# A list schedule that keeps VectorE and GpSimd apart on SBUF operands, in a two-layer hybrid encoder

## The chip, the cores and the metric

One core of a Trainium2 chip runs the whole program once. The metric is the device time in microseconds (us) of one execution, the median of several; lower is better. Engines are named as in the profile: PE (TensorE matmuls), PEld (its weight loads), DVE (VectorE), ACT (ScalarE), POOL (GpSimd), SP (SyncE, which issues the DMAs here).

## The reference

Two encoder layers on x of 512 tokens by 1024 features, float32. Cut to what is computed:

```python
for l in range(2):
    x = x + 0.5 * swiglu(rms_norm(x, ffn1_norm[l]), ffn1_w_gate[l], ffn1_w_up[l], ffn1_w_down[l])
    h = rms_norm(x, mix_norm[l])
    pa, pb, pc, pd = jnp.split(h @ w_in[l], IN_SPLITS, axis=-1)
    ya = neighbourhood_mixer(pa, ...)   # 4 heads, 8 x 16 window of an 8 x 64 grid, bias
    yb = mla_mixer(pb, ...)             # 4 heads, low-rank q and kv, rope
    yc = diff_mixer(pc, ...)            # 4 heads, two softmaxes each, T5 bias
    yd = gqa_mixer(pd, ...)             # 4 query heads on 2 kv heads, axial rope
    x = x + jnp.concatenate([ya, yb, yc, yd], axis=-1) @ w_out[l]
    x = x + 0.5 * swiglu(rms_norm(x, ffn2_norm[l]), ffn2_w_gate[l], ffn2_w_up[l], ffn2_w_down[l])
    x = rms_norm(x, final_norm[l])
```

The feed-forward width is 2816.

## The kernel before, in words

Activations lie transposed, features on the 128 partitions and the 512 tokens along the free dimension. Every float32 product is made from float32r operands that are split into a high half (a cast, on ACT) and a low half (source minus high half, a subtraction): three matmuls hi*hi, hi*lo, lo*hi. So each weight that comes in by DMA costs one ACT cast and one subtraction of up to 1024 columns. In the feed-forward stages the subtractions are DVE's. In the mixing stage (`mix`, once per layer) the subtractions of the projection weights (`pieces`, `divide`, `split`) are POOL's, as are two products of each rope (`do_rope`), the reciprocal roots of up to four columns (`rsqrt`), some memsets, and, ahead of the first mixing stage, the building of the masked bias tables (`masked`). All else of that kind is DVE's: the low halves of activations and probabilities, the softmax's row maxima and negations (`nm`), Newton steps of larger reciprocal roots (`rt`, `ri`), norms and residual additions.

The mixing stage runs the projections as generators (`Filler`) between 64 softmax steps. A step is: scores on PE, row maximum and its negation `nm` on DVE, exponential on ACT, four transposes on PE, their copies by ACT and DVE, and the product with the values on PE. So PE, DVE and ACT hand each step to one another.

The program order of all this is only a starting rank. The class `Plan` records every instruction with its queue (0 DVE, 1 ACT, 2 POOL, 3 PE, 4 SP), finds the dependencies from the boxes that instructions read and write, gives each a modelled cost (`cost`) and lag, and then places all of them on a model of the five queues (`schedule`): at each step it takes the queue that can start soonest and there the ready instruction of the lowest rank. It does so forward, then three times backward and forward, each pass ranked by the times of the one before. At the end the instructions are issued in the order of their modelled starts (`issue`). That fixes the order on each engine; on the chip an engine runs its instructions in that order, each as soon as its semaphores allow. In the model of before, queues hold one another up only through dependencies; a POOL instruction and a DVE instruction never do otherwise.

All instructions carry the line of the helper that issues them, L204, so groups are told apart by operation and tile. Tile names: `bank` is PSUM; `plain` and `round` are the SBUF arenas of float32 and float32r; `x`, `R`, `kr` and the small tiles are in SBUF.

Of the kernel before, what the change touches and what calls it, by code (L numbers as in the profile page):

```python
# [45 lines left out]
class Plan:  # L46
# [83 lines left out]
        return max(0.65, outs[0].nbytes() / 360e3)  # L130

    @staticmethod
    def schedule(queue, rank, costs, before, after):

        left, when, starts = [len(b) for b in before], [0.0] * len(queue), [0.0] * len(queue)
        coming, ready, free = [[] for _ in range(5)], [[] for _ in range(5)], [0.0] * 5
        for i, n in enumerate(left):
            if not n:
                heapq.heappush(coming[queue[i]], (0.0, i))
        for _ in queue:  # L140
            t, q = min((free[q] if ready[q] else max(free[q], coming[q][0][0]), q) for q in range(5) if ready[q] or coming[q])
            while coming[q] and coming[q][0][0] <= t:
                i = heapq.heappop(coming[q])[1]
                heapq.heappush(ready[q], (rank[i], i))
            i = heapq.heappop(ready[q])[1]
            starts[i] = t
            free[q] = t + costs[i]
            for j, lag in after[i]:
                when[j] = max(when[j], free[q] + lag)
                left[j] -= 1  # L150
                if not left[j]:
                    heapq.heappush(coming[queue[j]], (when[j], j))
        return starts

    def issue(self):
        ops, self.ops = self.ops, None
        writes, reads, deps, costs, tails, reads_of, turn = {}, {}, [], [], [], [], {}

        def over(a, b):
            return a[0] < b[1] and b[0] < a[1] and a[2] < b[3] and b[2] < a[3]  # L160

        def inside(a, b):
            return b[0] <= a[0] and a[1] <= b[1] and b[2] <= a[2] and a[3] <= b[3]

        for i, (q, _, _, name, a, kw, pin) in enumerate(ops):
            outs, ins = self.operands(a, kw)
            costs.append(self.cost(q, name, outs, ins, kw))
            tails.append(0.65 + min(0.65, outs[0].nbytes() / 360e3) if q == 4 else 0.0)
            wr, rd = [b for o in outs for b in self.boxes(o)], [b for o in ins for b in self.boxes(o)]
            d = {j for t, r in rd for b, j in writes.get(t, ()) if over(r, b)}  # L170
            reads_of.append(set(d))
            for t, r in wr:
                d.update(j for b, j in writes.get(t, []) + reads.get(t, []) if over(r, b))
            for t, r in rd:
                reads.setdefault(t, []).append((r, i))
            for t, r in wr:
                writes[t] = [e for e in writes.get(t, []) if not inside(e[0], r)] + [(r, i)]
                reads[t] = [e for e in reads.get(t, []) if not inside(e[0], r)]
            if q == 3:
                d |= {turn[wr[0][0]]} if wr[0][0] in turn else set()  # L180
                turn[wr[0][0]] = i
            if pin is not None:
                d.add(pin)
            d.discard(i)
            deps.append(d)
        before, after = [[] for _ in ops], [[] for _ in ops]
        for i, d in enumerate(deps):
            for j in d:
                q = ops[j][0]
                lag = tails[j] + (self.LATENCY[q] if q != ops[i][0] or q < 3 and j in reads_of[i] else 0.0)  # L190
                lag += self.REFILL if ops[i][0] == 3 != q else 0.0
                before[i].append((j, lag))
                after[j].append((i, lag))
        queue = [o[0] for o in ops]
        starts = self.schedule(queue, [o[1] for o in ops], costs, before, after)
        for _ in range(3):
            ends = [-(t + c) for t, c in zip(starts, costs)]
            back = self.schedule(queue, ends, costs, after, before)
            starts = self.schedule(queue, [-(t + c) for t, c in zip(back, costs)], costs, before, after)
        order = sorted((t, i) for i, t in enumerate(starts))  # L200
        with self.tc.manual_schedule():
            for _, i in order:
                call, a, kw = ops[i][2], *ops[i][4:6]
                call(*a, **kw)  # L204
# [1534 lines left out]
```

## Time and profile before

| | us |
|---|---|
| median of 3 runs | 2082.45 |
| lowest and highest of them | 2078.38, 2082.48 |
| profiled execution | 2078.18 |
| its span, first to last instruction | 2076.4 |
| PE busy in the span | 2012.1 (97%) |
| DVE busy | 1560.9 (75%) |
| ACT busy | 993.3 (48%) |
| POOL busy | 185.7 (9%) |
| mean granted TensorE clock | 0.988 of full |

The stages follow one another: feed-forward 1 of layer 0 up to about 340 us, mixing up to about 700, two feed-forwards (layer 0's second, layer 1's first) up to about 1360, mixing of layer 1 up to about 1720, the last feed-forward and the output norm. POOL is busy almost only in and just before the two mixing stages. A busy time counts an instruction from its start to its end, also while it is held up by something inside the engine, so an instruction of a few columns that shows 2 us has been held; idle time in front of an instruction is a wait for a semaphore.

### The profile page before, as it was taken

To read this page: it belongs to the slowest core of one execution; us is meant where nothing else is said; L and a number is where in the kernel's file an instruction comes from. 1 tells how busy PE (TensorE), PEld (TensorE's weight loads), DVE (VectorE), ACT (ScalarE), POOL (GpSimd) and SP (SyncE) were. 2 spreads that over 40 slices of the span, in tenths; PEclk is the share of its full clock that TensorE was granted. 3 is DMA by queue.
4 is the path that set the end of the run, shared out by engine and by line. 5 is a ranking of instruction groups with operands and counts; after the bars stand their busy time and mean duration, and the time that the engine had idled before them with its cause. 6 is when DMAs were issued, how large, how long until landed. Compare 5 with 4: busy or idle time off the path is not lost.

```text
span 2076.4 us, 30904 instructions
## 1 busy us (share of the span) xinstructions
PE 2012.1 (97%) x12072; PEld 1779.0 (86%) x12072; DVE 1560.9 (75%) x2553; ACT 993.3 (48%) x1575; POOL 185.7 (9%) x147
## 2 busy tenths in 40 slices
PE   8999999989999999999999999999899999999997
PEld 7989888767788898988899898987678889989896
DVE  8957767597867995775899495775978789859575
ACT  6524424466765652442554243345666665425232
POOL 0000032233210000000000000012331100000000
PEclk9999999999999999999999999999999999999998
DMA  4443445443324233232414223253532441423322
GB/s 151 132 135 114 132 145 185 136 123 105 98 66 140 85 123 101 82 122 75 139 52 135 79 89 126 74 168 111 152 96 75 119 135 56 128 71 104 120 75 78
DMA packets 90666, 230.12 MB, mean 111 GB/s; under 512 B 9844, under 2 KB 24820, under 8 KB 90520
## 3 DMA queue, kind: packets, MB, share of 16 engines
q1 hardware_dynamic: 90520, 228.15, 35.4%
q8 instruction: 95, 1.56, 0.3%
q14 instruction: 51, 0.42, 0.1%
HBM read 192.83 MB, written 14.27 MB: 100 GB/s over the span
## 4 chain that ended last, share of the span: by engine, by line
PE 78%; DVE 14%; DMA 3%; ACT 2%; issue 2%; SPq 0%; POOL 0%; POOLq 0%; DVEq 0%; ACTq 0%
PE bank L204 78%; DVE round L204 5%; DVE plain L204 4%; ACT round L204 1%; DMA plain<-in_wf_dram 1%; DVE x L204 1%; DVE nm L204 1%; ACT plain L204 1%; DMA plain<-in_win_dram 1%; DVE R L204 1%; DVE cc L204 0%; DVE rt L204 0%; SPq L204 0%; DVE mx L204 0%; POOL r L204 0%
## 5 line engine op out<-in xcount | busy, mean ns | idle before, releaser
L204 PE MATMUL bank<-round 128*128 128x256 f32 (+2 forms) x10812 | 1910.6, 336 | 35.4 <-DVE nm L204 15.0
L204 PEld LDWEIGHTS bank<-round 128*128 128x128 f32 x10812 | 1635.3, 191 | 239.9 <-DVE nm L204 20.7
L204 ACT CAST round<-plain 128x1024 fp32r<-128x1024 f32 (+2 forms) x576 | 540.7, 955 | 666.1 <-PE bank L204 435.2
L204 DVE TENSOR_TENSOR round<-plain,round 128x1024 fp32r<-128x1024 f32 (+2 forms) x532 | 584.7, 1117 | 112.6 <-ACT round L204 111.1
L204 DVE TENSOR_TENSOR plain<-plain 128x512 f32<-128x512 f32 (+2 forms) x442 | 290.0, 674 | 55.3 <-DMA plain<-in_wf_dram 34.2
L204 DVE TENSOR_TENSOR x<-x,bank 128x512 f32<-128x512 f32 x130 | 88.5, 684 | 164.6 <-PE bank L204 164.5
L204 ACT COPY plain<-bank 128x256 f32<-128x256 f32 (+2 forms) x240 | 96.4, 413 | 142.4 <-PE bank L204 82.7
L204 PEld LDWEIGHTS bank<-kr,plain 128*128 128x128 f32 x968 | 121.4, 167 | 31.4 <-DVE round L204 8.2
L204 PE MATMUL bank<-kr,plain 128*128 128x128 f32 (+3 forms) x968 | 136.1, 261 | 12.4 <-DVE round L204 6.7
L204 POOL TENSOR_TENSOR round<-plain,round 128x1024 fp32r<-128x1024 f32 (+2 forms) x44 | 102.4, 2328 | 361.7 <-ACT round L204 318.3
L204 DVE TENSOR_TENSOR plain<-bank,plain 128x256 f32<-128x256 f32 (+2 forms) x200 | 101.6, 515 | 26.5 <-PE bank L204 16.3
L204 DVE TENSOR_TENSOR round<-bank,round 128x512 fp32r<-128x512 f32 (+4 forms) x162 | 103.3, 644 | 24.3 <-ACT round L204 23.4
L204 ACT CAST round<-bank 128x512 fp32r<-128x512 f32 (+4 forms) x162 | 87.7, 552 | 54.9 <-PE bank L204 53.6
L204 ACT ACTIVATE plain<-plain 128x1024 f32<-128x1024 f32 (+1 forms) x64 | 59.3, 927 | 70.1 <-DVE plain L204 69.3
L204 POOL TENSOR_TENSOR r<-z,mhalf 128x4 f32<-128x4 f32 (+1 forms) x7 | 11.2, 1605 | 802.6 <-DVE z L204 802.1
L204 ACT ACTIVATE plain<-plain,nm 128x512 f32<-128x512 f32 (+2 forms) x96 | 64.1, 669 | 38.1 <-DVE nm L204 35.5
L204 DVE CUSTOM_DVE_ANT_0 plain<-bank,round 128x512 f32<-128x512 f32 (+2 forms) x96 | 58.4, 616 | 14.1 <-PE bank L204 9.9
L204 DVE TENSOR_REDUCE mx<-bank 128x1 f32<-128x512 f32 x64 | 43.9, 686 | 16.7 <-PE bank L204 16.0
L204 POOL MEMSET round<- 128x128 f32 (+1 forms) x36 | 8.1, 240 | 382.1 <-PE bank L204 376.9
L204 POOL TENSOR_TENSOR plain<-plain 128x256 f32<-128x256 f32 (+1 forms) x24 | 26.9, 1149 | 157.4 <-DVE x L204 126.4
L204 DVE TENSOR_TENSOR plain<-plain,R 128x1024 f32<-128x1024 f32 x32 | 39.1, 1222 | 0.5
L204 DVE SCALAR_TENSOR_TENSOR plain<-plain,R 128x1024 f32<-128x1024 f32 x32 | 39.1, 1221 | 0.4
(169 smaller groups left out, 680.6 us busy)
## 6 DMA issues: line engine op xcount, KB each, us to landing
plain<-in_wf_dram SPq DMA_DIRECT2D x176, 512.0 KB, 3.3
plain<-in_wd_dram SPq DMA_DIRECT2D x64, 512.0 KB, 4.1
plain<-in_win_dram SPq DMA_DIRECT2D x40, 512.0 KB, 3.5
round<-round SPq DMA_DIRECT2D x112, 128.0 KB, 2.4
plain<-in_wd_dram SPq DMA_DIRECT2D x32, 384.0 KB, 4.1
round<-round SPq DMA_DIRECT2D x40, 256.0 KB, 4.1
plain<-in_wout_dram SPq DMA_DIRECT2D x16, 384.0 KB, 2.9
xd<-x SPq DMA_DIRECT2D x16, 256.0 KB, 4.0
```

What stands on the lines that cost most here:

```text
L204: call(*a, **kw)
```

## The change

The scheduler gets a new rule. `shares` marks instructions all of whose operands are in SBUF: every POOL instruction but a memset, and on DVE `tensor_tensor`, `scalar_tensor_tensor`, `tensor_scalar` and `tensor_copy`. In every pass, forward and backward, a marked instruction starts in the model no sooner than the end of the marked one that was placed last, whichever of the two queues that was on (`held`). The choice of the next instruction of a queue is as it was: the rank decides, and a marked instruction that is chosen keeps its queue until it can start. No instruction is added, removed or given to another engine; only the modelled times, and with them the order on each engine, can differ.

```diff
+    def shares(q, name, outs, ins):
+
+        if any(ap.space != bass.MemoryType.SB for ap in outs + ins):
+            return False
+        return q == 2 and name != "memset" or q == 0 and name in ("tensor_tensor", "scalar_tensor_tensor", "tensor_scalar", "tensor_copy")
+
+    @staticmethod
+    def schedule(queue, rank, costs, before, after, shared):
+
+        held = 0.0
...
             i = heapq.heappop(ready[q])[1]
+            if shared[i]:
+                t = max(t, held)
+                held = t + costs[i]
             starts[i] = t
             free[q] = t + costs[i]
...
             costs.append(self.cost(q, name, outs, ins, kw))
+            shared.append(self.shares(q, name, outs, ins))
...
-        starts = self.schedule(queue, [o[1] for o in ops], costs, before, after)
+        starts = self.schedule(queue, [o[1] for o in ops], costs, before, after, shared)
         for _ in range(3):
             ends = [-(t + c) for t, c in zip(starts, costs)]
-            back = self.schedule(queue, ends, costs, after, before)
-            starts = self.schedule(queue, [-(t + c) for t, c in zip(back, costs)], costs, before, after)
+            back = self.schedule(queue, ends, costs, after, before, shared)
+            starts = self.schedule(queue, [-(t + c) for t, c in zip(back, costs)], costs, before, after, shared)
```

## Rows read from the trace of the kernel before

**Rows 1.** The page, busy time of each engine, share of the span, instructions.

```profile
PE 2012.1 (97%) x12072; PEld 1779.0 (86%) x12072; DVE 1560.9 (75%) x2553; ACT 993.3 (48%) x1575; POOL 185.7 (9%) x147
```

**Rows 2.** Stretches: length, busy PE PEld DVE ACT POOL, granted clock, DMA share, GB/s.

```profile
340.00:700.00 360.00, 339.71 (x1829) 284.79 (x1829) 277.30 (x619) 217.23 (x415) 78.66 (x58) 0.97 0.42 120
700.00:1360.00 660.00, 658.82 (x4187) 599.90 (x4186) 498.11 (x654) 276.98 (x370) 7.05 (x5) 1.00 0.31 99
1360.00:1720.00 360.00, 340.78 (x1843) 286.32 (x1842) 276.22 (x617) 217.01 (x416) 71.98 (x52) 0.98 0.41 118
```

**Rows 3.** PE's waits from 340 to 700: total us, times, longest.

```profile
PE bank L204 <- DVE nm L204: 7.5, 5, 1.9
PE bank L204 <- DVE round L204: 6.2, 5, 2.1
PE bank L204 <- ACT round L204: 1.7, 1, 1.7
PE bank L204 <- DVE x L204: 1.5, 1, 1.5
```

**Rows 4.** PE's waits from 1360 to 1720, the same columns.

```profile
PE bank L204 <- DVE round L204: 3.3, 2, 2.1
PE bank L204 <- DVE R L204: 2.3, 1, 2.3
```

**Rows 5.** POOL in order of time: start, length, engine, operation, tiles, wait before.

```profile
440.52 2.40 POOL L204 TENSOR_TENSOR round<-plain,round 128x1024 fp32r<-128x1024 f32 x1 [7.61 <-ACT round L204]
477.77 2.53 POOL L204 TENSOR_TENSOR round<-plain,round 128x1024 fp32r<-128x1024 f32 x1 [4.27 <-DMA round<-round]
527.82 2.40 POOL L204 TENSOR_TENSOR round<-plain,round 128x1024 fp32r<-128x1024 f32 x1 [2.94 <-PE bank L204]
```

**Rows 6.** DVE in order of time, beside those.

```profile
441.00 2.47 DVE L204 TENSOR_TENSOR round<-plain,round 128x512 fp32r<-128x512 f32 x1 [0.99 <-ACT round L204]
...
477.97 2.35 DVE L204 TENSOR_TENSOR rt<-dz,dr 128x8 f32<-128x8 f32 x1
480.36 0.17 DVE L204 SCALAR_TENSOR_TENSOR rt<-rt,dr 128x8 f32<-128x8 f32 x1
...
481.24 0.68 DVE L204 CUSTOM_DVE_ANT_0 plain<-bank,round 128x512 f32<-128x512 f32 x1
...
528.01 2.25 DVE L204 TENSOR_SCALAR ri<-zb 128x32 int32<-128x32 int32 x1
530.18 0.68 DVE L204 TENSOR_REDUCE mx<-bank 128x1 f32<-128x512 f32 x1
```

**Rows 7.** PE in order of time, after those.

```profile
444.73 1.95 PE L204 MATMUL bank<-kr,plain 128*128 128x2 f32 x16 [1.27 <-DVE round L204]
...
481.99 0.73 PE L204 MATMUL bank<-round 128*128 128x512 f32 x2 [1.26 <-DVE nm L204]
482.55 0.60 PE L204 MATMUL bank<-kr,plain 128*128 128x128 f32 x4
482.90 1.39 PE L204 MATMUL bank<-round 128*128 128x512 f32 x5
...
532.79 0.66 PE L204 MATMUL bank<-kr,plain 128*128 128x128 f32 x4 [2.06 <-DVE round L204]
```

**Rows 8.** DVE's groups by shape from 340 to 700: busy us, mean ns.

```profile
L204 DVE TENSOR_TENSOR nm<-mx,bn 128x1 f32<-128x1 f32 x16 | 6.5, 408 | 0.2
...
L204 DVE TENSOR_TENSOR nm<-mx,d1n 128x1 f32<-128x1 f32 x8 | 1.6, 194 | 0.1
```

**Rows 9.** Stretches of 10 us, columns as in rows 2.

```profile
450.00:460.00 10.00, 7.33 (x26) 5.04 (x26) 9.21 (x29) 4.63 (x10) 2.41 (x1) 0.83 0.91 235
530.00:540.00 10.00, 7.93 (x40) 6.54 (x39) 8.34 (x29) 4.73 (x10) 0.22 (x1) 0.83 0.40 107
570.00:580.00 10.00, 10.00 (x45) 8.02 (x45) 6.44 (x20) 3.26 (x7) 1.01 (x1) 0.77 0.00 0
1550.00:1560.00 10.00, 7.93 (x42) 6.69 (x41) 8.39 (x23) 4.62 (x10) 1.11 (x1) 0.83 0.40 105
```

More of the change, by code (lines that the diff above doesn't have):

```diff
@@ L132, in schedule @@
     @staticmethod
-    def schedule(queue, rank, costs, before, after):
+    def shares(q, name, outs, ins):
[5 more added lines that the diff above has]
+        held = 0.0
         left, when, starts = [len(b) for b in before], [0.0] * len(queue), [0.0] * len(queue)
@@ L156, in issue @@
         ops, self.ops = self.ops, None
-        writes, reads, deps, costs, tails, reads_of, turn = {}, {}, [], [], [], [], {}
+        writes, reads, deps, costs, tails, reads_of, turn, shared = {}, {}, [], [], [], [], {}, []
         def over(a, b):
```

## The prediction, made before the changed kernel ran

> **What bounds the kernel now.** I began with the busy times of the page: PE is busy 2012.1 of 2076.4 us [rows 1], so PE is the bound, and what an order can win is PE's idle time and what the granted clock loses, 2076.4 - 2012.1 = 64.3 us of idle at most. The order changes only where POOL works, so the second view was the table of stretches by stage [rows 2]. It shows where the idle time lies: 360 - 339.7 = 20.3 us in the first mixing stage, 360 - 340.8 = 19.2 us in the second, and only 660 - 658.8 = 1.2 us in the two feed-forwards between them, which POOL hardly touches. The reader should also see there that the granted clock is 0.97 and 0.98 in the mixing stages and 1.00 between them: 0.03 x 360 + 0.02 x 360 = 18 us, an estimate from these rows, are lost to stretches at the lower of the clock's two levels (1.2 instead of 2.4 GHz).
>
> Third, what PE waits for in the mixing stages [rows 3, 4]: small instructions of DVE, 1 to 2 us at a time. Fourth, and decisive, the engines side by side in order of time. A POOL subtraction runs from 440.52 to 442.92, and the DVE subtraction that starts in it at 441.00 shows 2.47 us and ends half a microsecond after it. Another POOL subtraction runs from 477.77 to 480.30; a DVE product of 8 columns that begins at 477.97 takes 2.35 us, the next one of the same size 0.17. At 527.82 it is again so, with a DVE `tensor_scalar` of 32 columns that takes 2.25 us [rows 5, 6]. An instruction with a PSUM operand keeps its 0.68 us. So a DVE instruction with SBUF operands stands still until the POOL instruction is done, and what is queued behind it on DVE is late. PE then waits 1.27, 1.26 and 2.06 us [rows 7]. The groups by shape say the same: the negation `nm` takes 194 ns in the mean in one head group and 408 ns in another [rows 8].
>
> The Trainium skill, "SBUF — State Buffer", section "Who interferes with whom", has the rule: the two engines share a port pair as an exclusive lock, and whichever comes second is blocked for the whole instruction. This case's trace agrees, with the 2.35 us above.
>
> **The change part by part.** Nothing is added, removed or moved to another engine, so the busy times of PE, ACT and POOL should stay as they are but for holds. POOL's 78.7 and 72.0 us [rows 2] still shut DVE out whenever they meet. So the holds themselves cost what they did. What changes is that the model now knows of them. Before, it placed a dependent PE instruction right behind the modelled end of the DVE chain; on the chip the chain ends up to 2.3 us later, and PE, which goes in order, stands. With the holds in the model, PE is seen to be free there and the schedule can put another ready matmul in that place.
>
> What this can win is PE's waits behind holds. I followed the waits of the first mixing stage one by one to the DVE instruction that ended them: nearly all of those on `nm`, `round`, `x` and on ACT's `round` have a held instruction in front. They sum to 7.5 + 6.2 + 1.7 + 1.5 = 16.9 us [rows 3]. In the second stage `nm`, ACT's `round` and `x` wait the same, and `round` 3.3 [rows 4]: 14.0 us. I leave out the 2.3 us on `R` there, as a DMA is also late in front of it. The sum is 30.9 us in 21 waits, 1.5 us each.
>
> How much of it comes back no row shows; I bound it from both sides. The upper end is all of it: between the mixing stages, where the modelled costs meet no hold, PE idles 0.2% although DVE is as full (498 of 660 us, 75%, against 277 of 360, 77%) [rows 2]. And there is work to put in: right behind the waits stand matmuls of projection weights, as the 1.39 us at 482.90 [rows 7]. The lower end is nothing: a hold must be met in the run where the model has it. POOL starts when an ACT cast, a DMA or a PE instruction lets it [rows 5], and some tenths of a microsecond decide which DVE instruction stands behind it. A hold that hits another instruction than planned costs its 1.5 us as before; one that was planned and doesn't come costs nothing, as PE is then full with the other work. The rows speak for both, so I take half: -15.5 us.
>
> The clock: three stretches with such waits were granted 0.83 [rows 9], which loses 0.17 x 10 = 1.7 us each, 5.1 us together. If half the waits go, half of this: -2.6, say -3 us. But at 570 to 580 us the clock was 0.77 with PE busy throughout [rows 9], so it also falls without idle time; I count on no more. Upper end: half of the 18 us, -9.
>
> Edits with one answer: the orders in the feed-forwards move little, since no marked POOL instruction of weight is there (7.05 us of POOL in 660 [rows 2]), and PE, full to 1.2 us, covers what does move; without that cover each would cost its hold, about 1.5 us. The DMAs' issue order follows the modelled starts and moves by at most the same couple of microseconds against weights fetched far ahead. The marking costs nothing on the chip; it is done before launch.
>
> The sum is -15.5 - 3 = -18.5 us on the profiled execution of 2078.2, so 2059.7. The median of before lies 4.3 us above that execution; put against it, 2082.45 - 18.5 = 2064.
>
> **The rivals.**
>
> *Nearly all comes back.* The schedule fills the holds as well as it fills the feed-forwards: -28 to -31 us of waits and -6 to -9 us of clock, about 2082 - 37 = 2045. For it: DVE's like load in the stage without waits. Against: holds shift against the plan.
>
> *First come stays first come.* The model sees the hold but doesn't avoid it: a POOL subtraction that is ready a moment before an urgent `nm` still goes first, in the plan as on the chip, and if PE has nothing whose operands and buffers are ready, it waits in the plan too. Then the time is that of before, 2082 within 4 us. For it: the choice of an instruction looks only at rank, and a chosen marked instruction keeps its queue. Against: the matmuls seen behind the waits. The Trainium skill, "SBUF — State Buffer", section "Summary: rules for kernel authors", says to schedule the instruction off the critical path when the two engines run at once; the change has no such choice, and by that rule nothing would be won here. To this rival also belongs that the changed order is hardly another one.
>
> *Slower: the new order meets more holds where it hurts.* POOL has 58 and 52 instructions in the two stages [rows 2], and PE waits behind some 21 holds now. With a new order on DVE they fall on other instructions. If the plan packs other matmuls into holds that don't come, the matmuls of the softmax chain come later, DVE and ACT stand, and the chain of 64 steps has less room when the next hold strikes. The price is 1.5 us a wait: above 21 exposed holds it is a loss, and with a third more, 28, it is 10 us, with the clock's 1.7 us in two or three stretches 14 us: 2096.
>
> **How the numbers follow.** A difference of 0.2%, 4 us, is about what a measurement can tell from none. Forecast (half, -8 to -28 us): 0.41, 2064, its own range 2054 to 2074. Nearly all: 0.20. No change: 0.16. Slower: 0.23. So faster 0.61, same 0.16, slower 0.23. The range that holds 8 in 10 goes from 2042, short of the best end of the first rival, to 2094, short of the worst of the last.
>
> **What would show it.** In the stretches of the two mixing stages PE's idle time falls from 39.5 to about 22 us, with the same counts of matmuls and POOL's busy time within a few microseconds. DVE instructions of a few columns that take 2 us are still there, but PE works through them. The waits on `nm` and `round` shrink. The feed-forwards take as long as before. The forecast is wrong if the held DVE instructions are as many and PE's waits behind them sum to 30 us or more; or if PE's idle time goes and the time stays, because the stages then end on the softmax chain and not on PE.

## The result, and the profile after

The changed kernel takes 2015.18 us (median; 2013.38 to 2021.46), the one before, beside it, 2080.41 us (2077.61 to 2082.48). The ratio is 0.9693, with a 95% interval of 0.9671 to 0.9715: 3.1% or 65 us faster. Forecast were 2064 us and a range of 2042 to 2094. The direction was right, the size more than three times too small, and the time lies outside the range.

The profiled execution of the changed kernel took 2016.73 us, 61.5 less than that of before. In all engines' busy times, the counterpart of [rows 1], the counts are the same, and PE has 28 us less to be busy with although its 12072 matmuls are the same:

```profile
PE 1984.0 (98%) x12072; PEld 1767.3 (88%) x12072; DVE 1552.6 (77%) x2553; ACT 993.3 (49%) x1575; POOL 186.3 (9%) x147
```

To see where the time went, the stretches have to hold the same work in both kernels. I cut them where POOL clears its tiles at the start of a mixing stage and where it takes the reciprocal root for the feed-forward behind it: mixing of layer 0, two feed-forwards, mixing of layer 1. Columns as in [rows 2]. The kernel before:

```profile
331.21:709.53 378.32, 358.03 (x1925) 300.30 (x1924) 293.44 (x642) 225.01 (x425) 79.72 (x61) 0.97 0.41 120
709.53:1355.83 646.30, 645.12 (x4112) 587.98 (x4111) 485.09 (x634) 270.00 (x359) 6.00 (x3) 1.00 0.31 99
1355.83:1730.34 374.51, 355.29 (x1922) 298.89 (x1922) 290.05 (x638) 224.81 (x425) 73.03 (x54) 0.98 0.40 117
```

and after:

```profile
331.30:676.38 345.08, 343.84 (x1932) 295.04 (x1931) 292.44 (x644) 224.50 (x425) 82.02 (x61) 1.00 0.45 131
676.38:1321.04 644.66, 643.27 (x4105) 586.65 (x4104) 482.37 (x633) 270.18 (x359) 4.54 (x4) 1.00 0.31 99
1321.04:1670.91 349.87, 346.52 (x1929) 295.86 (x1929) 289.49 (x640) 223.92 (x425) 73.72 (x55) 1.00 0.43 125
```

The mixing stages are 33.2 and 24.6 us shorter, 57.9 together; the feed-forwards between them 1.6. PE's idle time in the mixing stages falls from 20.3 + 19.2 = 39.5 to 1.2 + 3.4 = 4.6 us: 34.9 of the 57.9. The rest is 23.0 us less PE busy time for the same matmuls (each stretch holds 7 more after than before), and the granted clock has gone from 0.97 and 0.98 to 1.00. Added up over stretches of 10 us, where the rounding to two digits counts for less, the clock takes 10.2 and 8.5 us before, and 0 and 1.7 us after (one stretch of the second stage at 0.83): 17 of the 23 us. The other 6 us no run explains. Of DVE's busy time in these stages hardly anything is gone (293.4 and 292.4, 290.1 and 289.5 us), nor of POOL's.

What PE waits for in the two mixing stages after, in place of [rows 3, 4], is one line for the first stage and three for the second:

```profile
PE bank L216 <- DVE round L216: 1.2, 1, 1.2
...
PE bank L216 <- DVE R L216: 2.7, 1, 2.7
PE bank L216 <- DVE plain L216: 0.3, 1, 0.3
PE bank L216 <- POOL round L216: 0.3, 1, 0.3
```

And yet the holds are there. Two of them in order of time (start, length, engine, operation, tiles), first POOL, in place of [rows 5]:

```profile
411.95 2.41 POOL L216 TENSOR_TENSOR round<-plain,round 128x1024 fp32r<-128x1024 f32 x1 [7.64 <-ACT round L216]
...
549.38 2.87 POOL L216 TENSOR_TENSOR round<-plain,round 128x1024 fp32r<-128x1024 f32 x1
```

then DVE, in place of [rows 6]: a product of one column that stands for 2.02 us and one of 16 columns for 2.37 us, each until POOL's subtraction is about done,

```profile
412.35 2.02 DVE L216 SCALAR_TENSOR_TENSOR cc<-cc,lam,ss 128x1 f32<-128x1 f32 x1
414.30 0.68 DVE L216 CUSTOM_DVE_ANT_0 plain<-bank,round 128x512 f32<-128x512 f32 x1
...
549.31 0.68 DVE L216 TENSOR_TENSOR round<-plain,round 128x512 fp32r<-128x512 f32 x1
549.91 2.37 DVE L216 TENSOR_TENSOR F<-frs,fy 128x16 f32<-128x16 f32 x1
552.85 0.69 DVE L216 TENSOR_REDUCE mx<-bank 128x1 f32<-128x512 f32 x1 [0.57 <-PE bank L216]
```

and PE, in place of [rows 7]: 22 and 26 matmuls of 512 columns, without a pause, right across both holds.

```profile
411.75 4.51 PE L216 MATMUL bank<-round 128*128 128x512 f32 x22
416.10 0.60 PE L216 MATMUL bank<-kr,plain 128*128 128x128 f32 x4
...
547.67 5.38 PE L216 MATMUL bank<-round 128*128 128x512 f32 x26
552.89 0.60 PE L216 MATMUL bank<-kr,F 128*4 128x128 f32 x4
```

In the first mixing stage the holds also fall on other instructions. DVE's groups by shape there (busy us, mean ns), before,

```profile
L204 DVE TENSOR_TENSOR nm<-mx,bn 128x1 f32<-128x1 f32 x16 | 6.5, 408 | 0.2
L204 DVE TENSOR_TENSOR plain<-plain 128x512 f32<-128x512 f32 x6 | 5.1, 854 | 0.0
...
L204 DVE SCALAR_TENSOR_TENSOR rt<-rt,dr 128x16 f32<-128x16 f32 x3 | 0.5, 166 | 0.0
```

and after:

```profile
L216 DVE TENSOR_TENSOR plain<-plain 128x512 f32<-128x512 f32 x7 | 10.1, 1447 | 0.6 <-POOL plain L216 0.6
...
L216 DVE SCALAR_TENSOR_TENSOR rt<-rt,dr 128x16 f32<-128x16 f32 x3 | 4.3, 1423 | 0.0
L216 DVE TENSOR_TENSOR nm<-mx,bn 128x1 f32<-128x1 f32 x16 | 3.7, 234 | 0.2
```

`nm`, on which the exponential and then PE wait, is held less there (408 to 234 ns in [rows 8]'s terms), the rope's sums and a Newton step more. The second mixing stage shows that this isn't needed for the gain. Two of the three groups of `nm` in it, before and after:

```profile
L204 DVE TENSOR_TENSOR nm<-mx,bn 128x1 f32<-128x1 f32 x16 | 6.5, 409 | 0.2
L204 DVE TENSOR_TENSOR nm<-mx,d1n 128x1 f32<-128x1 f32 x8 | 1.5, 192 | 0.1
...
L216 DVE TENSOR_TENSOR nm<-mx,bn 128x1 f32<-128x1 f32 x16 | 6.2, 390 | 0.2
L216 DVE TENSOR_TENSOR nm<-mx,d1n 128x1 f32<-128x1 f32 x8 | 3.3, 411 | 0.0
```

With the third group, `nm` takes 11.6 us of DVE before and 12.5 after, and yet this stage is 24.6 us shorter and PE waits for no `nm` in it. One held `nm` of this stage in either kernel shows how. Before, ACT's exponential waits for it, ACT's casts come late behind that, and PE stands for 1.70 us:

```profile
1609.66 2.37 POOL L204 TENSOR_TENSOR round<-plain,round 128x1024 fp32r<-128x1024 f32 x1 [17.41 <-ACT round L204]
1610.01 2.04 DVE L204 TENSOR_TENSOR nm<-mx,bn 128x1 f32<-128x1 f32 x1
1612.08 0.78 ACT L204 ACTIVATE plain<-bank,nm,bp 128x512 f32<-128x512 f32 x1 [2.50 <-DVE nm L204]
1613.47 0.39 PE L204 MATMUL bank<-round 128*128 128x256 f32 x1 [1.70 <-ACT round L204]
```

After, the hold is as long, and PE goes on with other matmuls:

```profile
1544.22 2.39 POOL L216 TENSOR_TENSOR round<-plain,round 128x1024 fp32r<-128x1024 f32 x1 [2.41 <-ACT round L216]
1544.59 2.05 DVE L216 TENSOR_TENSOR nm<-mx,bn 128x1 f32<-128x1 f32 x1
1544.13 1.87 PE L216 MATMUL bank<-round 128*128 128x512 f32 x7
1545.84 0.60 PE L216 MATMUL bank<-kr,plain 128*128 128x128 f32 x4
1546.20 1.64 PE L216 MATMUL bank<-round 128*128 128x512 f32 x6
```

### The profile page after: what moved, and what is told of

It is laid out like the page before. It is cut to its first block, busy times and chain, and to the rows that moved or that the text cites. A ratio compares the mean times of both kernels' runs of the same rounds, so it can differ in the third digit from the quotient of the medians.

```text
span 2014.9 us, 30935 instructions
## 1 busy us (share of the span) xinstructions
PE 1984.0 (98%) x12072; PEld 1767.3 (88%) x12072; DVE 1552.6 (77%) x2553; ACT 993.3 (49%) x1575; POOL 186.3 (9%) x147
## 4 chain that ended last, share of the span: by engine, by line
PE 91%; DVE 5%; DMA 2%; issue 1%; ACT 1%; SPq 0%; POOLq 0%; POOL 0%; DVEq 0%; ACTq 0%
PE bank L216 91%; DVE round L216 2%; DVE plain L216 2%; DMA plain<-in_wf_dram 1%; ACT round L216 1%; DMA plain<-in_win_dram 1%; DVE x L216 0%; DMA round<-nab 0%; DMA x<-in_xT_dram 0%; DMA plain<-in_wd_dram 0%; DMA xd<-x 0%; ACT plain L216 0%; SPq L216 0%; DVE dr L216 0%; DVE cc L216 0%
## 5 line engine op out<-in xcount | busy, mean ns | idle before, releaser
L216 PE MATMUL bank<-round 128*128 128x256 f32 (+3 forms) x10812 | 1893.9, 334 | 16.1 <-ACT round L216 11.8
L216 PEld LDWEIGHTS bank<-round 128*128 128x128 f32 (+1 forms) x10812 | 1625.5, 190 | 208.0 <-ACT round L216 11.9
```

## The experiments

So two things could be at work, PE filling the holds (theory A) and, in the first stage at least, DVE's holds falling where nobody waits (theory B). The third candidate is that the order of before was an unlucky one and any other would have won (theory C). All medians, with the ratio to the kernel before on the same chip:

| run | holds in the model | median us | ratio, 95% interval |
|---|---|---|---|
| changed kernel | yes | 2015.2 | 0.9693 (0.9671 to 0.9715) |
| pe_order_only | yes, PE's order alone is new | 2059.3 | 0.9894 (0.9863 to 0.9925) |
| pe_dve_order | yes, PE's and DVE's | 2051.1 | 0.9864 (0.985 to 0.9879) |
| pe_dve_act_order | yes, PE's, DVE's and ACT's | 2029.6 | 0.9739 (0.9704 to 0.9775) |
| all_but_pe | yes, PE's order of before | 2079.2 | 0.9993 (0.9976 to 1.001) |
| hold_dve | DVE waits for POOL only | 2030.5 | 0.9757 (0.9733 to 0.978) |
| hold_pool | POOL waits for DVE only | 2074.1 | 0.9967 (0.9953 to 0.9981) |
| wrong_marks | on the wrong instructions | 2061.3 | 0.9898 (0.9866 to 0.9929) |
| uniform | no, DVE 12% longer | 2069.9 | 0.9937 (0.9915 to 0.996) |
| weights_dve | no, their cause mostly taken away | 2044.6 | 0.9822 (0.9799 to 0.9845) |
| perturb | no, another order | 2067.9 | 0.9932 (0.9911 to 0.9953) |
| perturb_rule | yes, another order | 2025.5 | 0.9741 (0.9727 to 0.9756) |
| perturb2 | no, another order | 2073.4 | 0.9962 (0.9945 to 0.9979) |
| perturb2_rule | yes, another order | 2023.3 | 0.9716 (0.9689 to 0.9743) |
| bypass | yes, and worked around | 2020.9 | 0.9718 (0.9704 to 0.9733) |
| pool_cost | yes, POOL's cost as measured | 2032.8 | 0.9781 (0.9764 to 0.9797) |

**Which engine's order.** After a schedule without holds, the orders of the other engines are kept as chains of dependencies, and the passes are repeated with the holds for the rest:

```diff
+        starts = [o[1] for o in ops]
+        for free, marks in ((range(5), [False] * len(ops)), ((3,), shared)):
+            last = {}
+            for i in sorted(range(len(ops)), key=lambda i: (starts[i], i)):
+                if queue[i] not in free:
+                    if queue[i] in last:
+                        before[i].append((last[queue[i]], 0.0))
+                        after[last[queue[i]]].append((i, 0.0))
+                    last[queue[i]] = i
+            starts = self.schedule(queue, starts, costs, before, after, marks)
...
```

> The order of DVE, ACT, POOL and SP is that of the kernel before; only PE's order is placed anew, with the holds in the model. Theory A (the gain is PE's order: other matmuls stand where DVE is held, and the holds stay) expects nearly all of the gain, 2015 to 2035 us, PE idle in the mixing stages under 10 us instead of 39.5, and the small DVE instructions (nm, rt) held as long as before. Theory B (the gain is DVE's order: the holds fall on instructions that nobody waits for) expects 2065 to 2085 us, since nm is held as before and PE has nothing to do meanwhile.

It took 2059 us, a third of the gain, between A and B. What PE waits for in this run shows why it isn't more:

```profile
PE bank L225 <- DVE nm L225: 16.4, 10, 3.2
PE bank L225 <- ACT round L225: 10.0, 1, 10.0
PE bank L225 <- DVE round L225: 4.5, 10, 0.8
```

In the old DVE order `nm` is as late as before, and PE waits for it 16.4 us in the whole span (15.0 before). (The 10 us on ACT are the start of the kernel.) The other way round, with `(0, 1, 2, 4)` in place of `(3,)`:

> The order of PE is that of the kernel before; DVE, ACT, POOL and SP are placed anew with the holds in the model. Theory A (the gain is PE's order) expects 2065 to 2090 us: PE still meets the late DVE results in the old order. Theory B (the gain is DVE's order, which lets holds fall where nobody waits) expects most of the gain, 2015 to 2035 us, with nm held for less than 250 ns in the mean instead of 408.

Nothing is gained, 2079 us: what theory A expected. This edit also binds DVE, though, since DVE has to serve PE's matmuls in the old order; the mean of `nm` in the group of [rows 8] with 408 ns stays at 407 ns. Then DVE together with PE, `(0, 3)`, and with ACT, `(0, 1, 3)`:

> The orders of ACT, POOL and SP are those of the kernel before; PE and DVE are placed anew with the holds in the model. PE alone gave 2059 us, all but PE 2079. The theory that PE and DVE have to be ordered together expects most of the gain, 2015 to 2040 us. If the times at which ACT's casts let POOL start have to move as well, it stays near PE alone, 2045 to 2060 us.

> Only the orders of POOL and SP are those of the kernel before; PE, DVE and ACT are placed anew with the holds in the model. If ACT's order (the casts that start POOL's subtractions) is what PE and DVE together (2051 us) still lack, most of the gain is there, 2015 to 2035 us. If it is the order in which POOL's work and the DMAs are issued, it stays at 2040 to 2055 us.

PE and DVE together bring 2051 us, little more than PE alone; with ACT's order it is 2030 us. So neither A nor B alone is right. The gain needs PE, DVE and ACT placed together. Why DVE's and ACT's orders have to change with PE's no run shows. What is left to 2015 us, with POOL's and the DMAs' order, is 14 us, little more than what two orders of the same kind differ by (below). Little of it is idle time: PE idles 2029.1 - 1996.3 = 32.8 us in the whole span of this run and 30.9 in the changed kernel's, but the mean granted clock of the two profiled executions is 0.990 and 0.996, which is some 12 us. (These four runs also start from the finished order of before and go through the passes twice; no run takes that by itself.)

**Which side of the rule.** In the model, only DVE waits for POOL, or only POOL for DVE:

```diff
-            if shared[i]:
-                t = max(t, held)
-                held = t + costs[i]
+            if shared[i] and q == 0:
+                t = max(t, held)
+            if shared[i] and q == 2:
+                held = t + costs[i]
```

> Half of the rule: in the model a marked DVE instruction waits for the POOL instruction placed last, but POOL never waits for DVE. The theory that the gain comes from the holds of DVE being known to the plan (PE and DVE ordered together around them) expects most of the gain, 2015 to 2040 us. If the gain needs the true exclusion of both sides, 2045 to 2075 us. The theory of an unlucky order of before makes no difference between this run and the next one.

> The other half: in the model POOL waits for the marked DVE instruction placed last, but DVE never waits for POOL, as in the kernel before. The theory that the holds of DVE have to be known expects little, 2060 to 2085 us, with PE idle 25 us or more in the mixing stages. The theory that POOL only has to be put off behind DVE's work expects most of the gain, 2015 to 2040 us.

2030.5 and 2074 us. Most of the gain, 50 us, lies in DVE's holds being known; putting POOL off behind DVE alone brings 0.3%.

**Is it this knowledge, or any other order?** The rule aimed at the DVE instructions that have a PSUM operand:

```diff
-        if any(ap.space != bass.MemoryType.SB for ap in outs + ins):
-            return False
-        return q == 2 and name != "memset" or q == 0 and name in (...)
+        if q == 0:
+            return any(ap.space != bass.MemoryType.SB for ap in outs + ins)
+        return q == 2 and name != "memset"
```

> The same rule as in the changed kernel, aimed at the wrong instructions: POOL's instructions and those DVE instructions that have a PSUM operand exclude one another in the model, those with SBUF operands alone don't. Both theories that the model gains by being true (A and B) expect no gain, 2070 to 2110 us, with PE idle 35 us or more in the mixing stages. Theory C (the order of before was an unlucky one, and any rule that keeps DVE and POOL apart, or any other order, wins as much) expects 2015 to 2045 us.

2061 us: a gain of 1% where A and B expected none, and PE idles 15.0 + 11.2 = 26 us in the mixing stages, where they expected 35 or more. Beside the mean of three orders without the rule, 2074 us (below), the gain is 13 us, about what these three differ by. A part of the reason may be that `nm` of this group isn't held in this order (row maxima, which read PSUM, are kept clear of POOL, and `nm` follows them); that is argued, not shown:

```profile
L216 DVE TENSOR_TENSOR nm<-mx,bn 128x1 f32<-128x1 f32 x32 | 5.0, 155 | 0.3
```

Its PE waits for other things in the whole span, 9.4 us on ACT's `plain` and 7.7 us on DVE's instead. The holds' time spread evenly over DVE's instructions:

```diff
-            return 0.069 + n / 960.0 * (1.1 if name == "scalar_tensor_tensor" and n > 32 else 1.0)
+            return 1.12 * (0.069 + n / 960.0 * (1.1 if name == "scalar_tensor_tensor" and n > 32 else 1.0))
```

> The scheduler of before without holds, but every DVE instruction is modelled 12% longer, about what the holds add to DVE's busy time in a mixing stage (31 of 277 us), spread evenly instead of set where they fall. Theories A and B (the place of the holds matters) expect a small part of the gain at most, 2055 to 2085 us. Theory C, and the idea that the plan only needs more slack for DVE, expect 2015 to 2040 us.

2070 us, as A and B expected. Then other orders, drawn by a lag that has nothing to do with holds, once without and once with the rule (`REFILL` 0.140 and 0.110 instead of 0.126):

> The scheduler of before without holds, with one modelled lag changed that has nothing to do with DVE or POOL (PE's refill 0.140 instead of 0.126): another order, drawn without any knowledge of the holds. The theory that the holds have to be known expects no gain beyond chance, 2065 to 2095 us. The theory of an unlucky order of before expects 2015 to 2050 us.

> The changed kernel with the same unrelated lag changed as in the run perturb (PE's refill 0.140 instead of 0.126): a second order drawn with the holds known, beside a second order drawn without (2068 us). If knowing the holds is worth its gain whatever the order, the distance to perturb stays 2% or more: 2010 to 2030 us. If the 2015 us of the changed kernel were a lucky draw, it falls back towards 2040 to 2065 us.

> A third order drawn without the holds: the scheduler of before with PE's refill at 0.110. If orders without the holds scatter by their luck around 2073 us, 2060 to 2090 us. If some of them reach the times of those with the rule, below 2045 us.

> A third order drawn with the holds: the changed kernel with PE's refill at 0.110. If the holds known are worth some 45 us whatever the order, 2010 to 2040 us, and 30 us or more below its partner without the rule. If the changed kernel's 2015 us is mostly luck, 2045 us or more.

With the two kernels of the case this makes three pairs: 2080.4 and 2015.2, 2067.9 and 2025.5, 2073.4 and 2023.3 us, so the rule is worth 65, 42 and 50 us, 53 in the mean. Orders of the same kind scatter by some 10 us: 12.5 in the three without the rule, 10.3 in the three with it. The one before happens to be the slowest of three, and the one after the fastest. Theory C explains that part, about 12 of the 65 us, and no more. (`pool_cost`, below, is a fourth order with the rule: 2033 us, 18 behind the fastest, and still 35 us ahead of the fastest without it.)

**The cause taken away.** The low halves of the projection weights are made on DVE, in the scheduler of before:

```diff
-            yield win[l, (0, 1, 2, 3, 4, 5, 6, 8, 9, 7, 10, 11, 12, 13, 14, 15, 16, 17, 18, 19)[i]], 1024, G
+            yield win[l, (0, 1, 2, 3, 4, 5, 6, 8, 9, 7, 10, 11, 12, 13, 14, 15, 16, 17, 18, 19)[i]], 1024, V
...
-                yield wuq[l], 768, G
-                yield wukv[l], 512, G
+                yield wuq[l], 768, V
+                yield wukv[l], 512, V
```

> The scheduler of before, without holds, but the cause is taken away: the low halves of the projection weights (22 subtractions of a mixing stage) are made on DVE instead of POOL, 1.22 us each instead of 2.40. If PE's waits and the lower clock in the mixing stages come from holds that the plan doesn't know, they go here as well: PE idle under 12 us in the two stages, 2020 to 2045 us. If the plan of before is short of something else (DVE's time in the mixing stages, or it was unlucky), the 2 x 27 us of additional DVE work make it no better, 2060 to 2110 us.

2044.6 us, at the edge of what was expected. The two mixing stages and one stretch of 10 us from the first (the latter without the other engines' columns):

```profile
330.37:691.35 360.98, 355.55 (x1925) 298.69 (x1924) 288.97 (x664) 224.92 (x425) 31.34 (x38) 0.98 0.43 126
1339.51:1699.72 360.21, 354.71 (x1924) 299.40 (x1924) 286.83 (x660) 225.05 (x425) 23.76 (x32) 0.98 0.42 121
...
550.00:560.00 10.00, 10.00 (x47) 0.66 0.14 39
```

DVE isn't busier than before, although it does 22 subtractions more in each stage: the holds that it no longer suffers pay for them. PE's idle time falls to 5.4 + 5.5 = 10.9 us, so the waits did come from holds. But the clock stays at 0.98, and a stretch is granted 0.66 while PE is busy throughout. The profiled execution is the slowest of the four, 2049.1 us at a mean clock of 0.988; the others took 2041 to 2045 us at 0.990 to 0.993. Of the 32 us between its span and the changed kernel's, 6 are idle time of PE and some 16 the clock (0.988 against 0.996).

**Two attempts at a better one.** In `bypass` a chosen instruction that is held lets the best ready unmarked one of its queue go first; in `pool_cost` the model's `n / 475.0` for POOL is `n / 455.0`, which is the 2.40 us of the trace.

```diff
+            if shared[i] and held > t:
+                other = min((e for e in ready[q] if not shared[e[1]]), default=None)
+                if other is not None:
+                    ready[q].remove(other)
+                    heapq.heapify(ready[q])
+                    heapq.heappush(ready[q], (rank[i], i))
+                    i = other[1]
```

> The changed kernel, and in the model an engine whose chosen instruction is held takes the best ready instruction that the rule does not mark instead. DVE then does work with PSUM operands while POOL runs. The theory that the held time of DVE, about 30 us in a mixing stage, still costs something expects 2000 to 2012 us. The theory that PE is the bound and its waits are already gone (4.6 us left in the two stages) expects no change, 2010 to 2025 us.

> The changed kernel with POOL's modelled cost set to what the trace shows (a subtraction of 1024 columns 2.40 us instead of 2.31). The theory that the gain grows with the truth of the modelled holds expects the same or a little better, 2005 to 2018 us. The theory that an order's luck weighs more than that expects anything from 2010 to 2035 us.

2021 and 2033 us: neither beats 2015. DVE is 12 us less busy with `bypass` (1540.1 us), and it doesn't help; that PE has next to no waits left to win fits this, but is argued. A model with a truer POOL cost is even slower. A difference of that size is not far outside the scatter of orders and says little about the edit itself.

## Why the prediction was right or wrong

**What bounds, and where.** Right. All but 3.6 of the 61.5 us between the profiles come from the two mixing stages, and PE's waits behind holds, with the clock that fell beside them, were what could go.

**Holds stay, PE works through them.** Right in the trace (the three holds above, DVE's unchanged busy time), but incomplete. I thought of PE's order alone: "the schedule can put another ready matmul in that place". PE alone won 20 us; DVE's and ACT's orders have to change with it. That the holds move off `nm` can't be the whole reason, as the second mixing stage gains without it.

**"So I take half: -15.5 us."** This is the step that failed, and the term that was mis-sized most: 34.9 of 39.5 us of idle time went, 88%. I had the row for it, the feed-forwards where a plan with true costs leaves PE idle 0.2%, and set against it the worry that some tenths of a microsecond decide which instruction is held: "A hold that hits another instruction than planned costs its 1.5 us as before." The runs show little of that cost: of the 30.9 us of waits that I counted, one of 1.2 us on `round` is left in the first mixing stage and none in the second. Orders with the rule do differ, by 10 us and with `pool_cost` by 18, but part of that is the clock; none loses half of the gain. Of the 8.6 us of idle time that I had left out, more than half went as well. The wait on `R` in the second stage did not: 2.3 us before, 2.7 after.

**The clock, "-2.6, say -3 us".** It gave 17. I counted only stretches with a wait in them and took the fall at 570 to 580 us, with PE busy, as a sign that the rest would stay. It didn't: the first mixing stage now runs at full clock throughout, the second loses 1.7 us. My upper end for it, half of the 18 us, excluded the measured value, and so even the best rival, 2045, fell 30 us short.

**Feed-forwards.** Right: 1.6 us for two of them.

**The rivals.** "Nearly all comes back" was the case, given 0.20, with its clock term too small. "First come stays first come" is refuted: the choice among ready instructions is as it was, and the waits are gone. The Trainium skill, "SBUF — State Buffer", section "Summary: rules for kernel authors", says to schedule whichever instruction is off the critical path when the two engines would meet. I had drawn from it that nothing would be won here. This order follows that advice in part, without choosing to, in the first mixing stage (`nm` 408 to 234 ns) and not in the second, and in both what is still held is covered by PE's other work. "Slower" had its mechanism in the trace, holds that fall on other instructions, but PE hardly waited behind them.

**The range.** It was built round a middle that one row contradicted. The chance for the rival that this row spoke for should have been the largest, and the scatter between orders, which I could have allowed for on either side, belongs in it as 10 to 20 us.

## What to carry to other kernels

Where an order is fixed ahead by a model, look in the trace for instructions that take far longer than their size: each may be a conflict that the model doesn't know, and an engine that waits behind it is losing time that other work could fill. Putting the conflict into the model can win nearly all of that without removing any of it, provided the bound engine has other work ready and the orders of all the engines that hand work to one another are made anew together. Before reading anything into a few tenths of a percent between two such orders, draw a second and a third order by an unrelated small change: here that alone moved the time by 7 to 12 us.

## What the runs showed of the hardware that was not expected

The clock weighed half as much as the waits. With idle time of 20.3 and 19.2 us in the mixing stages it was granted at 0.97 and 0.98, with 1.2 and 3.4 us at 1.00, for the same matmuls. But idle time is not the whole of it. In `perturb`, with 19.5 and 15.4 us of idle time, it was 0.99. With the weights' subtractions on DVE it was 0.98 at 5.4 us of idle time, and down to 0.66 for 10 us in which PE never paused, that is, for two thirds of them at the lower of its two levels. Just before and into that stretch, from 548.2 to 552.9 us, 33 of PE's 36 matmuls were small ones of 128 columns on `kr` and `plain`:

```profile
548.21 2.39 PE L204 MATMUL bank<-kr,plain 128*128 128x128 f32 x21
550.47 0.94 PE L204 MATMUL bank<-round 96*128 96x512 f32 x3
551.25 1.65 PE L204 MATMUL bank<-kr,plain 128*128 128x128 f32 x12
```

Whether that has to do with it was not tried, and stays open. Nor is the clock set by the order alone: of 16 executions of the kernel before on one chip, the fastest, 2073.9 us, had a mean clock of 0.990 and the slowest, 2090.2 us, 0.983.

The holds are blind to size: a product of one column (2.02 us) and one of 16 (2.37 us) both stood until POOL's subtraction ended, and a `tensor_scalar` with a single SBUF input was held as well [rows 6]. They also go the other way. POOL's subtraction at 549.38 took 2.87 us instead of 2.40; a DVE subtraction with SBUF operands alone had begun just before it, at 549.31.
